# Results of the first five pairs of experts: to DRAM by slot and fetched by token, in place of products with the table of places

## The chip, the cores and the metric

The kernel runs on one core of one Trainium2 chip. The metric is the device time of one execution in microseconds (us), the median of several runs; lower is better. On the core, TensorE (PE in the profile) multiplies matrices, VectorE (DVE), ScalarE (ACT) and GpSimd (POOL) work element by element, and SyncE (SP) issues most transfers. Transfers run on 16 DMA engines. Those that SP issues are queue q1 in the profile, those that POOL issues are q0.

## The reference

The model has two layers. Each has a mixer (attention and gated linear attention), which the change does not touch, and a mixture of experts over 512 tokens of 1024 numbers. For each token a router chooses one of 4 groups and in it 2 of 8 experts, with a weight for each. What matters here is the sum over the experts:

```python
comb = (jax.nn.one_hot(grp_idx[:, 0], N_GROUPS, dtype=f32)[:, :, None]
        * exp_w[:, None, :]).astype(h.dtype)
y = jnp.zeros_like(hf)
for g in range(N_GROUPS):
    a = jnp.einsum('nd,edf->nef', hf, w_gate[g])
    u = jnp.einsum('nd,edf->nef', hf, w_up[g])
    y = y + jnp.einsum('nef,efd->nd', jax.nn.silu(a) * u * comb[:, g, :, None], w_down[g])
```

Afterwards x + gate_f * y is the input of the next layer or the output. All is float32. Each of the 32 experts of a layer has 3 MiB of weights (gate, up and down), 96 MiB in a layer. 512 tokens make 1024 choices of an expert.

## The kernel before

The mixture is `moe`. Each expert has 64 places (slots) for tokens; expert e's place s is slot 64e + s. The experts go in 16 pairs, 128 slots each, and pair i holds slots 128i to 128i + 127. The stage has these steps for pair i; the names in brackets are the tiles under which the profile lists them.

- `fetch` (L977, tile `rows`): POOL issues an indirect transfer of the normed token rows of the pair from DRAM, by a list of tokens for each slot. Empty slots have an index that is out of bounds and are left out.
- `gather` (L997, tile `g`): PE transposes the rows, and ACT and DVE scale them into `gT`.
- `hidden` (tiles `gu`, `hs`): 16 products of 64 columns against 512, for both experts of the pair, then silu and a product. Written below as gu(i).
- `turn` (L1032, tile `hsT`): PE transposes `hs`, ACT copies it to `hT`.
- `down` (tile `d`): 8 products with the down weights, d(i). DVE multiplies by the weight of the slot and by gate_f (L1057, tile `o`); ACT rounds this to a high part (L1062, `ohi`), and POOL makes the rest (L1063, `olo`).
- `places` (L1080, L1082): DVE makes the table `oT`, which has a one where a token holds a slot of the pair.
- `combine`: for each of 8 units (4 blocks of 128 tokens by 2 halves of 512 columns) PE multiplies the table with `ohi` and `olo` (tile `y`, L78), and DVE adds the result to x (L1070). So a pair has 16 products `y` and 8 additions, whatever number of tokens it holds.

The loop over i issues, for each pair, d(i-1), then gu(i), then the 8 units of pair i-1, between which lie the transposes of a later gather and the `turn` of pair i. The last two pairs are combined together in `combine_last`. PE's order around this is the program's (`pm` and `keep_in_program_order`); on DVE, ACT and POOL a scheduler may move instructions.

Weights come through two sets of buffers: 5 of 2 MiB (gate and up of one expert, tile `wgu`, L884) and 4 of 1 MiB (down, tile `wd`, L880). SP issues the loads in one fixed order, and a load waits at the head of SP's queue until the products that read its buffer are done. Nine loads are issued before the stage begins. After gu(0) come gate and up of experts 5 and 6, whose buffers gu(0) gives back, then down of experts 4 and 5, whose buffers d(0) gives back, and so on in the same manner. The last three are gate and up of expert 31, and down of experts 30 and 31.

`overflow_lists` (L1147 to L1176) prepares lists for experts with more than 64 tokens; it is issued after gu(1). In this data no expert has more, and the loop that would serve them runs no time.

Of the kernel before, what the change touches and what calls it, by code (L numbers as in the profile page):

```python
# [9 lines left out]
F = mybir.dt.float32  # L10
R = mybir.dt.float32r
BF = mybir.dt.bfloat16
I32 = mybir.dt.int32
# [7 lines left out]
P = 128  # L21
# [2 lines left out]
SBW, GKW, GVW, RANK, NIN = 512, 256, 512, 16, 3088  # L24
NE, FE, CAP = 32, 256, 64
NX = 16


@with_exitstack
def hybrid_decoder_kernel(ctx, tc, x, c, w_ada, b_ada, norm_mix, norm_ffn, w_in, w_gk2, b_gk, q_gain,  # L30
# [180 lines left out]

    xs = dram.tile([S, D], F, name="xs")
    xg = dram.tile([S, D], F, name="xg")

    mod = [const.tile([P, 6, KT], F, name=f"mod{l}") for l in range(L)]
    gates, gms, rowt = {}, {}, {}
# [643 lines left out]
    def moe(l, xt, ss, pool):  # L860
# [176 lines left out]
        def down(hT, ws, i=None):  # L1037

            n = len(ws)
            r = slice(0, 64 * n)  # L1040
            parts, last = [], None
            if i == NE // 2 - 1:

                last = wgu([P, 2, 2, 512], R, name="last")
            for q in range(2):
                pd = bank("d", "dy", 4)
                for j in range(2):
                    for e in range(n):
                        pm(pd[64 * e:64 * e + 64], hT[:, j, 64 * e:64 * e + 64],
                           ws[e][:, D * j + 512 * q:D * j + 512 * q + 512], j == 0, j == 1)  # L1050
                o = ot([P, 512], name="o")
                gate = gates[l, 5][r, 512 * q:512 * q + 512]
                if i is None:
                    V.tensor_tensor(o[r], pd[r], gate, op=OP.mult)
                    parts.append(o)
                else:
                    V.scalar_tensor_tensor(o, pd, cws[:, i:i + 1], gate, op0=OP.mult, op1=OP.mult)  # L1057
                    if last is not None:
                        hi, lo = last[:, q, 0], last[:, q, 1]
                    else:  # L1060
                        hi, lo = ohl([P, 512], R, name="ohi"), ohl([P, 512], R, name="olo")
                    A.activation(hi, o, AF.Copy)  # L1062
                    (G if last is None else V).tensor_tensor(lo, o, hi.bitcast(F), op=OP.subtract)  # L1063
                    parts.append((hi, lo))
            return parts
# [29 lines left out]
        def combine_last(pairs):  # L1095

            order = [units[u] for u in (0, 2, 4, 6, 1, 3, 5, 7)]
            tags = [("dy", 4), ("dy", 4), ("g", 2), ("g", 2), ("gu", 1), ("misc", 1), ("dy", 4), ("dy", 4)]
            ps = {}

            def unit(n, u):
                tt, q = order[u]
                if n == 0:
                    ps[u] = bank("y", *tags[u])
                oT, parts = pairs[n]
                for j in range(2):
                    pm(ps[u], oT[:, P * tt:P * tt + P], parts[q][j], n == 0 and j == 0, n == 1 and j == 1)
                if n:
                    add(tt, q, ps[u], True)

            for u in range(5):
                unit(0, u)
            yield
            for n, u in ((0, 5), (0, 6), (1, 0), (1, 1), (0, 7), (1, 2), (1, 3), (1, 4), (1, 5), (1, 6), (1, 7)):
                unit(n, u)

        def spread(slot, slot0):

# [80 lines left out]
        with tc.issue_after(listed.ins), tc.issue_after(normed.ins):  # L1199
# [14 lines left out]
            V.tensor_tensor(e2, e2, den, op=OP.mult)  # L1214
            V.tensor_tensor(cw[:, :, 1:2], e2, gw, op=OP.mult)
            dump(f"cw{l}", cw)
            exw = tmp.rearrange("p t k e -> p (t k) e")
            V.tensor_tensor(exw, ex.rearrange("p t k e -> p (t k) e"), cw.rearrange("p t k -> p (t k)")[:, :, None].to_broadcast([P, NT * 2, NE]), op=OP.mult)
        cws = pool.tile([P, NE // 2], F, name="cws")
# [17 lines left out]
        for _ in rest:  # L1237
            pass
        gT1, second = gather(fetched[1:2])
        hs = None  # L1240
        for i in range(NE // 2):
            while not {(0, 2 * i), (0, 2 * i + 1)} <= set(loaded):
                load_weights(1)
            if i % 2 == 0:
                now = gT
                if i < NE // 2 - 2:
                    gT, rest = gather(fetched[i + 2:i + 4])
                    fetched += [fetch(idx[:, j:j + 1]) for j in range(i + 4, min(i + 6, NE // 2))]

            if i:  # L1250
                part = places(i - 1), down(hT, [loaded.pop((1, e)) for e in (2 * i - 2, 2 * i - 1)], i - 1)
            *_, hs = hidden(gT1 if i == 1 else now, 0 if i < 2 else P * (i % 2), [loaded.pop((0, e)) for e in (2 * i, 2 * i + 1)])
            load_weights(4)
            if i == 1:
                overflow_lists()
            if i == NE // 2 - 1:
                break

            if i == 0:
                for _ in second:  # L1260
                    pass
                weights_by_slot()
            for u in range(4):
                for v in range(2):
                    if i:
                        combine(2 * u + v, *part)
                next(rest, None)
                if u == 2:
                    hT = turn(hs)
        last = []  # L1270
        end = combine_last([part, last])
        next(end)
# [93 lines left out]
```

## Time and profile before

| what | value |
|---|---|
| median of 3 runs | 1231.82 us (1229.91 to 1234.94) |
| the profiled execution | 1231.71 us, its span 1229.6 us |
| PE, DVE, ACT, POOL busy | 1176.4, 687.8, 472.6, 188.2 us |
| moved by DMA | 312.27 MB, mean 254 GB/s over the span |
| the expert stage, layer 0 | first gu at 375.15 us, last at 606.74 us |
| the expert stage, layer 1 | first gu at 969.53 us, last at 1201.12 us |

The page's second part cuts the span in 40 slices of 30.7 us. A busy PE says only that matmuls were under way; whether PE or the transfers set the pace is read from who waits for whom, and from the share of the 16 DMA engines in the same stretch. The GB/s of a slice counts all that moved.

### The profile page before, as it was taken

To read this page: it belongs to the slowest core of one execution; us is meant where nothing else is said; L and a number is where in the kernel's file an instruction comes from. 1 tells how busy PE (TensorE), PEld (TensorE's weight loads), DVE (VectorE), ACT (ScalarE), POOL (GpSimd) and SP (SyncE) were. 2 spreads that over 40 slices of the span, in tenths; PEclk is the share of its full clock that TensorE was granted. 3 is DMA by queue.
4 is the path that set the end of the run, shared out by engine and by line. 5 is a ranking of instruction groups with operands and counts; after the bars stand their busy time and mean duration, and the time that the engine had idled before them with its cause. 6 is when DMAs were issued, how large, how long until landed. Compare 5 with 4: busy or idle time off the path is not lost. (4 is left out here: it accounts for less than half of the span.)

```text
span 1229.6 us, 17212 instructions
## 1 busy us (share of the span) xinstructions
PE 1176.4 (96%) x6441; PEld 743.4 (60%) x6441; DVE 687.8 (56%) x1343; ACT 472.6 (38%) x940; POOL 188.2 (15%) x222
## 2 busy tenths in 40 slices
PE   4999999999989999999999997999999999999996
PEld 2687766666765444444478785666776744444443
DVE  4475545465864555555566563445846565555553
ACT  4376646453242111111155764454624411111111
POOL 1000010011302222221110001001310222222110
PEclk8999999999999999999999999999999999999999
DMA  9653665643687999999445354564129599999981
GB/s 299 211 181 110 202 166 155 198 152 96 258 353 265 410 411 420 420 419 418 178 168 167 96 172 108 171 179 127 56 103 383 212 397 420 420 418 420 420 328 69
DMA packets 105902, 312.27 MB, mean 254 GB/s; under 512 B 12852, under 2 KB 49912, under 8 KB 81240
## 3 DMA queue, kind: packets, MB, share of 16 engines
q1 hardware_dynamic: 96920, 289.62, 63.3%
q0 software_dynamic: 8896, 21.52, 5.2%
q8 instruction: 52, 0.85, 0.3%
q14 instruction: 34, 0.28, 0.1%
HBM read 311.08 MB, written 8.40 MB: 260 GB/s over the span
## 5 line engine op out<-in xcount | busy, mean ns | idle before, releaser
L78 PE MATMUL gu<-wgu,gT 128*64 128x512 f32 x1024 | 225.4, 592 | 0.1
L74 PE MATMUL proj<-whl,hh 128*128 128x512 f32 (+2 forms) x768 | 220.6, 370 | 0.1
L78 PEld LDWEIGHTS gu<-wgu,gT 128*64 128x64 f32 x1024 | 75.4, 137 | 143.7 <-issue 142.2
L74 PEld LDWEIGHTS proj<-whl,hh 128*128 128x128 f32 x768 | 133.9, 190 | 35.0 <-issue 13.3
L1070 DVE TENSOR_TENSOR x<-y,x 128x512 f32<-128x512 f32 x240 | 148.2, 679 | 0.9 <-PE y L78 0.9
L74 PE MATMUL proj<-whl,hl 128*128 128x512 f32 (+2 forms) x384 | 138.6, 362 | 0.0
L1025 DVE TENSOR_TENSOR hs<-hs,gu 128x256 f32<-128x256 f32 x32 | 13.5, 421 | 201.2 <-ACT hs L1024 201.2
L78 PE MATMUL d<-wd,hT 128*64 128x512 f32 x512 | 116.9, 598 | 1.4 <-ACT hT L1034 1.4
L1063 POOL TENSOR_TENSOR olo<-o,ohi 128x512 fp32r<-128x512 f32 x60 | 77.0, 1285 | 263.4 <-ACT ohi L1062 263.4
L96 DVE TENSOR_TENSOR whl<-raw,whl 128x512 fp32r<-128x512 f32 (+2 forms) x128 | 73.2, 574 | 78.0 <-ACT whl L95 67.6
L78 PE MATMUL y<-ohi,oT 128*128 128x512 f32 x240 | 104.5, 436 | 0.0
L95 ACT ACTIVATE whl<-raw 128x512 fp32r<-128x512 f32 (+2 forms) x128 | 66.4, 524 | 76.6 <-PE proj L74 64.7
L78 PE MATMUL y<-olo,oT 128*128 128x512 f32 x240 | 94.2, 393 | 0.0
L74 PEld LDWEIGHTS proj<-whl,hl 128*128 128x128 f32 x384 | 72.4, 189 | 14.2 <-issue 4.3
L1024 ACT ACTIVATE hs<-gu 128x256 f32<-128x256 f32 x32 | 12.3, 385 | 168.4 <-PE gu L78 168.4
L78 PEld LDWEIGHTS d<-wd,hT 128*64 128x64 f32 x512 | 33.9, 136 | 62.2 <-issue 48.1
L78 PEld LDWEIGHTS y<-ohi,oT 128*128 128x128 f32 x240 | 45.4, 189 | 31.7 <-issue 26.0
L1003 ACT ACTIVATE gT<-g,mod 128x256 f32<-128x256 f32 (+1 forms) x72 | 39.0, 544 | 62.6 <-DVE gT L1005 62.3
L1062 ACT ACTIVATE ohi<-o 128x512 fp32r<-128x512 f32 x60 | 37.8, 630 | 61.7 <-DVE o L1057 61.7
L1057 DVE SCALAR_TENSOR_TENSOR o<-d,cws,gate_f 128x512 f32<-128x512 f32 x64 | 47.6, 746 | 21.4 <-PE d L78 21.4
L733 POOL TENSOR_TENSOR raw<-raw,gate_m 128x1024 f32<-128x1024 f32 x16 | 40.4, 2533 | 122.9 <-DMA raw<-in_w_out_dram 63.1
L78 PE MATMUL ada<-wada,ct 128*32 128x512 f32 x320 | 50.2, 600 | 5.3 <-DMA wada<-in_w_ada_dram 3.8
(332 smaller groups left out, 1935.0 us busy)
## 6 DMA issues: line engine op xcount, KB each, us to landing
wgu<-in_w_gate_dram SPq DMA_DIRECT2D x64, 1024.0 KB, 9.6
wgu<-in_w_up_dram SPq DMA_DIRECT2D x64, 1024.0 KB, 11.8
wd<-in_w_down_dram SPq DMA_DIRECT2D x64, 1024.0 KB, 11.0
wada<-in_w_ada_dram SPq DMA_DIRECT2D x96, 512.0 KB, 5.1
raw<-in_w_in_dram SPq DMA_DIRECT2D x80, 256.0 KB, 4.5
raw<-in_w_out_dram SPq DMA_DIRECT2D x16, 512.0 KB, 5.0
raw<-in_w_in_dram SPq DMA_DIRECT2D x32, 128.0 KB, 4.0
xg<-xn POOLq DMA_DIRECT2D x8, 512.0 KB, 5.9
```

The source lines that it names most:

```text
L74: T.matmul(o, a, b, start=start, stop=stop, skip_group_check=True)
L78: tc.keep_in_program_order(T.matmul(o, a, b, start=start, stop=stop, skip_group_check=True))
L95: A.activation(hi, src, AF.Copy)
L96: eng.tensor_tensor(lo, src, hi.bitcast(F), op=OP.subtract)
L733: G.tensor_tensor(t, t, gates[l, 2][:, None, cols].to_broadcast([P, 2, 512]), op=OP.mult)
L1003: A.activation(o, src, AF.Identity, scale=m, bias=b)
L1024: A.activation(hs[r], gu[r, 0:256], AF.Silu)
L1025: V.tensor_tensor(hs[r], hs[r], gu[r, 256:512], op=OP.mult)
L1057: V.scalar_tensor_tensor(o, pd, cws[:, i:i + 1], gate, op0=OP.mult, op1=OP.mult)
L1062: A.activation(hi, o, AF.Copy)
L1063: (G if last is None else V).tensor_tensor(lo, o, hi.bitcast(F), op=OP.subtract)
L1070: V.tensor_tensor(xc, ps, xc, op=OP.add)
```

## The change

The outputs `o` of pairs 0 to 4 (NY = 5) are no longer split into two parts and multiplied with the table of places. POOL writes them to a DRAM tensor `ys` of 640 rows, row = slot, in two transfers of 128 rows of 2 KB for each pair. Near the end of the stage (from pair 12 on) POOL fetches rows of `ys` by token: for each block of 128 tokens and each of the 2 choices one indirect transfer into `back`, 8 in a layer. A choice whose slot is 640 or more is out of bounds and is left out. DVE then adds `back` times a mask (`ysm`, 1 or 0) to x, 128x1024 at a time.

The order of the first pairs changes with it: gu(i) comes first, then `turn` of pair i-1, 8 transposes, then d(i-1).

```diff
+NY = 5
...
+    ys = dram.tile([NY * P, D], F, name="ys")
...
-                o = ot([P, 512], name="o")
+                o = (ohl if i is not None and i < NY else ot)([P, 512], name="o")
...
                     V.scalar_tensor_tensor(o, pd, cws[:, i:i + 1], gate, op0=OP.mult, op1=OP.mult)
+                    if i < NY:
+                        kept_dma(G, ys[P * i:P * i + P, 512 * q:512 * q + 512], o)
+                        continue
...
+        ysi, ysm = pool.tile([P, NT, 2], I32, name="ysi"), t3(2, "ysm")
+
+        def take_back(tt, k):
+
+            r = rows_([P, D], name="back")
+            G.indirect_dma_start(r, None, ys[:, :], bass.IndirectOffsetOnAxis(ap=ysi[:, tt, k:k + 1], axis=0),
+                                 bounds_check=NY * P - 1, oob_is_err=False)
+            xc = xt[tt // 2][:, tt % 2]
+            return lambda: V.scalar_tensor_tensor(xc, r, ysm[:, tt, k:k + 1], xc, op0=OP.mult, op1=OP.add)
...
+            V.tensor_scalar(ysi, slot, 65535.0, None, op0=OP.min)
+            V.tensor_scalar(ysm, slot, float(NY * P), None, op0=OP.is_lt)
...
-            if i:
+            if i > NY:
                 part = places(i - 1), down(hT, [loaded.pop((1, e)) for e in (2 * i - 2, 2 * i - 1)], i - 1)
-            *_, hs = hidden(gT1 if i == 1 else now, 0 if i < 2 else P * (i % 2), [loaded.pop((0, e)) for e in (2 * i, 2 * i + 1)])
+            *_, new = hidden(gT1 if i == 1 else now, 0 if i < 2 else P * (i % 2), [loaded.pop((0, e)) for e in (2 * i, 2 * i + 1)])
             load_weights(4)
...
+            if i <= NY:
+                if i:
+                    hT = turn(hs)
+                for _ in range(4):
+                    next(rest, None)
+                if i:
+                    down(hT, [loaded.pop((1, e)) for e in (2 * i - 2, 2 * i - 1)], i - 1)
+                hs = new
+                if i == NY:
+                    hT = turn(hs)
+                continue
+            hs = new
             for u in range(4):
                 for v in range(2):
-                    if i:
-                        combine(2 * u + v, *part)
+                    combine(2 * u + v, *part)
+                if i >= NE // 2 - 4 and u % 2 == 0:
+                    taken.append(take_back(*back.pop(0)))
+                    if len(taken) > 1:
+                        taken.pop(0)()
                 next(rest, None)
                 if u == 2:
                     hT = turn(hs)
+        for (tt, k) in back:
+            taken.append(take_back(tt, k))
+        for add_back in taken:
+            add_back()
```

The order of SP's instructions is the same in both kernels, and outside the expert stages no engine's order changes. Three places matter below. The first is PE at the start of the stage, from gu(0) on. Before:

```order
L78 MATMUL gu<-wgu,gT 64x512 x16
L997 MATMUL g<-ident,rows 128x128 x8
L78 MATMUL lst<-tmp,ohp 64x16 x16
L78 MATMUL slots<-dg,n_72 128x128 x8
L997 MATMUL g<-ident,rows 128x128 x6
L1032 MATMUL hsT<-ident,hs 128x128 x2
L997 MATMUL g<-ident,rows 128x128 x2
L78 MATMUL d<-wd,hT 64x512 x8
L78 MATMUL gu<-wgu,gT 64x512 x16
```

In the changed kernel the same stretch, up to gu(2):

```order
L80 MATMUL gu<-wgu,gT 64x512 x16
L1000 MATMUL g<-ident,rows 128x128 x8
L80 MATMUL lst<-tmp,ohp 64x16 x16
L80 MATMUL slots<-dg,n_72 128x128 x8
L1000 MATMUL g<-ident,rows 128x128 x8
L80 MATMUL gu<-wgu,gT 64x512 x16
L1035 MATMUL hsT<-ident,hs 128x128 x2
L1000 MATMUL g<-ident,rows 128x128 x8
L80 MATMUL d<-wd,hT 64x512 x8
L80 MATMUL gu<-wgu,gT 64x512 x16
```

The first `d`, which gives back two `wd` buffers, now stands behind gu(1) instead of ahead of it.

The second place is POOL near the end of the stage of layer 0, from the third of the new fetches on; a number behind a name tells instances apart. olo_4932 and olo_4943 belong to pair 12, olo_5047 and olo_5058 to pair 13, the last two to pair 14. Before, this stretch held the six `olo` alone.

```order
L1128 DMA back_4981<-ys_125,ysi_3539 128x1024
L1069 TENSOR_TENSOR olo_4932<-o_4929,ohi_4931 128x512
L1069 TENSOR_TENSOR olo_4943<-o_4940,ohi_4942 128x512
L1128 DMA back_5010<-ys_125,ysi_3539 128x1024
L1128 DMA back_5089<-ys_125,ysi_3539 128x1024
L1128 DMA back_5110<-ys_125,ysi_3539 128x1024
L1128 DMA back_5174<-ys_125,ysi_3539 128x1024
L1069 TENSOR_TENSOR olo_5047<-o_5044,ohi_5046 128x512
L1069 TENSOR_TENSOR olo_5058<-o_5055,ohi_5057 128x512
L1128 DMA back_5178<-ys_125,ysi_3539 128x1024
L1069 TENSOR_TENSOR olo_5140<-o_5137,ohi_5139 128x512
```

Six of the eight fetches stand among the `olo` of the last pairs. The third, fourth, seventh and eighth (back_4981, back_5010, back_5174, back_5178) wait for a buffer that DVE gives back when it has added the first, second, third and fourth.

The third place is DVE from the places of the tokens (`pos`) to the list of tokens (`idx`), on which the first fetch depends. Before:

```order
L960 TENSOR_REDUCE pos<-tmp 128x8
L963 SCALAR_TENSOR_TENSOR slot<-eid,pos 128x8
L964 TENSOR_SCALAR far<-pos 128x8
L1181 TENSOR_TENSOR ohp<-iota,pos 128x512
L965 SCALAR_TENSOR_TENSOR slot<-far,slot 128x8
L1155 TENSOR_TENSOR cq<-pos,thr 128x56
L1229 TENSOR_TENSOR dg<-ident,slot 128x512
L972 TENSOR_SCALAR idx<-nv 128x16
```

In the changed kernel:

```order
L963 TENSOR_REDUCE pos<-tmp 128x8
L1163 TENSOR_TENSOR cmp<-n_e,thr 128x224
L966 SCALAR_TENSOR_TENSOR slot<-eid,pos 128x8
L967 TENSOR_SCALAR far<-pos 128x8
L1197 TENSOR_TENSOR ohp<-iota,pos 128x512
L968 SCALAR_TENSOR_TENSOR slot<-far,slot 128x8
L1165 TENSOR_REDUCE extra<-cmp 128x32
L1247 TENSOR_TENSOR dg<-ident,slot 128x512
L975 TENSOR_SCALAR idx<-nv 128x16
```

`cmp` now stands ahead of `ohp`, and the rest of `overflow_lists` with the two new instructions (`ysi`, `ysm`) follows between `idx` and the first `gT`; before, `overflow_lists` lay behind gu(0).

## Rows read from the trace of the kernel before

**Rows 1.** The page's second part: the span in 40 slices, busy tenths of PE and of the DMA engines, and GB/s.

```profile
PE   4999999999989999999999997999999999999996
DMA  9653665643687999999445354564129599999981
GB/s 299 211 181 110 202 166 155 198 152 96 258 353 265 410 411 420 420 419 418 178 168 167 96 172 108 171 179 127 56 103 383 212 397 420 420 418 420 420 328 69
```

**Rows 2.** Busy time by stretch: start and end, length, then PE, PEld, DVE, ACT and POOL busy (x instructions), granted PE clock, share of the DMA engines, GB/s.

```profile
400.00:450.00 50.00, 50.00 (x243) 24.60 (x243) 29.68 (x52) 9.99 (x20) 11.69 (x10) 1.00 1.00 411
450.00:500.00 50.00, 50.00 (x242) 23.27 (x240) 28.92 (x52) 10.35 (x20) 12.03 (x11) 1.00 1.01 419
500.00:550.00 50.00, 50.00 (x241) 23.12 (x238) 26.20 (x46) 9.79 (x19) 11.87 (x10) 1.00 1.01 419
540.00:580.00 40.00, 40.00 (x194) 18.75 (x194) 23.58 (x42) 8.77 (x17) 7.66 (x6) 1.00 1.01 420
340.00:345.00 5.00, 5.00 (x25) 4.14 (x24) 2.72 (x5) 2.83 (x8) 0.00 (x0) 1.00 1.04 434
1220.00:1224.00 4.00, 0.31 (x2) 0.00 (x0) 2.12 (x4) 0.00 (x0) 0.00 (x0) 1.00 1.03 377
```

**Rows 3.** Waits, 370 to 610 us: all of PE's, then the two longest of SP's queue (300 to 600 us): who, for whom, us in total, times, longest.

```profile
PE g L997 <- DMA rows<-xg,idx: 0.8, 1, 0.8
PE d L78 <- ACT hT L1034: 0.2, 1, 0.2
...
SPq L884 <- PE gu L78: 109.9, 14, 33.7
SPq L880 <- PE d L78: 93.0, 14, 7.8
```

**Rows 4.** PE in order of time (start, length, instructions, count): the start of the stage, then pair 3 up to gu(4), and the last gu.

```profile
382.23 1.09 PE L997 MATMUL g<-ident,rows 128*128 128x128 f32 x8
386.84 0.40 PE L1032 MATMUL hsT<-ident,hs 128*128 128x128 f32 x2
387.70 3.65 PE L78 MATMUL d<-wd,hT 128*64 128x512 f32 x16 [0.24 <-ACT hT L1034]
391.19 7.04 PE L78 MATMUL gu<-wgu,gT 128*64 128x512 f32 x32
...
422.11 7.04 PE L78 MATMUL gu<-wgu,gT 128*64 128x512 f32 x32
429.07 0.50 PE L78 MATMUL y<-ohi,oT 128*128 128x512 f32 x1
434.08 3.65 PE L78 MATMUL d<-wd,hT 128*64 128x512 f32 x16
437.57 7.04 PE L78 MATMUL gu<-wgu,gT 128*64 128x512 f32 x32
...
606.74 7.04 PE L78 MATMUL gu<-wgu,gT 128*64 128x512 f32 x32
```

**Rows 5.** SP's issues in order of time: the first loads that wait for a buffer, and the last gate and up.

```profile
382.26 0.33 SPq L884 DMA_DIRECT2D wgu<-in_w_gate_dram  x1
391.38 0.80 SPq L880 DMA_DIRECT2D wd<-in_w_down_dram  x2
...
584.15 0.42 SPq L884 DMA_DIRECT2D wgu<-in_w_up_dram  x1
```

**Rows 6.** Transfers by issue: how many, KB each, median us from issue to landing. First those issued from 382 to 390 us, then from 391 to 398, from 530 to 537, and from 583 to 586.

```profile
wgu<-in_w_up_dram SPq DMA_DIRECT2D x2, 1024.0 KB, 9.6
...
wd<-in_w_down_dram SPq DMA_DIRECT2D x2, 1024.0 KB, 6.4
...
wd<-in_w_down_dram SPq DMA_DIRECT2D x2, 1024.0 KB, 12.5
...
wgu<-in_w_up_dram SPq DMA_DIRECT2D x1, 1024.0 KB, 10.0
```

**Rows 7.** DMA queues from 400 to 580 us: packets, MB, share of 16 engines; and the fetches issued there.

```profile
q1 hardware_dynamic: 9945, 72.48, 97.2%
q0 software_dynamic: 1440, 2.41, 3.6%
...
rows<-xg,idx POOLq DMA_INDIRECT x10, 9.5
```

**Rows 8.** DVE in order of time at the start of the stage (start, length, what, idle before and until what).

```profile
365.55 0.42 DVE L960 TENSOR_REDUCE pos<-tmp 128x8 f32<-128x256 f32 x1
366.16 0.69 DVE L1181 TENSOR_TENSOR ohp<-iota,pos 128x512 f32<-128x512 f32 x1
369.92 0.43 DVE L1218 TENSOR_TENSOR tmp<-ex,cw 128x256 f32<-128x256 f32 x1
374.68 1.78 DVE L1005 TENSOR_SCALAR gT<-g,mod 128x128 f32<-128x128 f32 x4 [4.33 <-PE g L997]
386.52 0.38 DVE L1147 TENSOR_TENSOR cmp<-n_e,thr 128x224 f32<-128x224 f32 x1
392.38 0.17 DVE L1167 TENSOR_SCALAR over<-over 128x8 f32<-128x8 f32 x1
```

**Rows 9.** The page's fifth part: one line's additions to x.

```profile
L1070 DVE TENSOR_TENSOR x<-y,x 128x512 f32<-128x512 f32 x240 | 148.2, 679 | 0.9 <-PE y L78 0.9
```

**Rows 10.** Stretches around a lull of PE ahead of the stage, columns as in Rows 2.

```profile
355.00:360.00 5.00, 2.60 (x13) 1.48 (x13) 2.41 (x9) 2.95 (x2) 0.50 (x1) 1.00 1.01 393
360.00:365.00 5.00, 4.52 (x35) 4.25 (x34) 4.30 (x21) 3.40 (x3) 1.09 (x3) 0.66 0.90 366
365.00:370.00 5.00, 4.63 (x63) 4.42 (x61) 4.31 (x22) 1.49 (x2) 0.42 (x1) 1.00 0.26 106
```

More of the change, by code (lines that the diff above doesn't have):

```diff
@@ L1239, in moe @@
         gT1, second = gather(fetched[1:2])
-        hs = None
+        hs, back, taken = None, [(tt, k) for tt in range(NT) for k in range(2)], []
         for i in range(NE // 2):
@@ L1262, in moe @@
                 weights_by_slot()
+            if i <= NY:
[9 more added lines that the diff above has]
+                continue
+            hs = new
             for u in range(4):
                 for v in range(2):
-                    if i:
-                        combine(2 * u + v, *part)
+                    combine(2 * u + v, *part)
[3 more added lines that the diff above has]
+                        taken.pop(0)()
                 next(rest, None)
```

## The prediction

> **What bounds the kernel now.** I read the page's second part first. In slices 13 to 19 and again in slices 33 to 38 (a slice is 30.7 us) PE is at 9 and the DMA engines are at 9 as well, with 410 to 420 GB/s [rows 1]. These are the two expert stages, and the change touches nothing else. The table of stretches says the same more sharply: from 400 to 550 us PE is busy 50.00 of 50 us and the share of the 16 DMA engines is 1.00 to 1.01 [rows 2]. So two resources are full at once, and the question is which has room. The list of waits answers for PE: from 370 to 610 us it waited 1.0 us in all, while SP's loads waited 203 us for PE's products to give buffers back [rows 3]. PE leads, and the weights follow. PE's rows give the pace: pair 3 from gu to gu takes 437.57 - 422.11 = 15.46 us [rows 4].
>
> But the weights follow closely. A pair needs 6 MiB, 6.29 MB; at the 420 GB/s of 540 to 580 us, which holds hardly anything but weights [rows 2], that is 15.0 us, and a fetch of rows costs more on top. The two loads of down weights issued at 391 us landed after 6.4 us, those issued at 530 us after 12.5 us [rows 6]: a backlog of some 6 us grew over the stage. The room that is left shows at the end: the up weights of expert 31 were issued at 584.15 us and took 10.0 us [rows 5, 6], so they were there at 594.2, and gu(15) read them from 606.74 [rows 4]. That is a slack of 12.6 us per layer, and it is all that PE can win before the weights are late.
>
> **The change part by part**, for layer 0; layer 1 repeats it.
>
> PE. A pair without products y saves this: from the end of gu(3) to d(3) it is 434.08 - 429.07 = 5.01 us [rows 4], and without the 16 y there remain 8 transposes (1.1 us for 8 by the row at 382.23) and a turn, 1.3 us together. That saves 3.7 us a pair, 18.5 us for five. If PE alone set the time, two layers would give 37 us.
>
> The weights at the start. PE's order shows d(0) moved behind gu(1). Before, d(0) ended at 391.2 and SP issued down of experts 4 and 5 at 391.38 [rows 4, 5]. Now gu(1) begins at 386.84 + 0.4 = 387.2 (where hsT stood, with two transposes left), takes 6.96 (422.11 to 429.07), then turn and transposes 1.3, d(0) 3.49 (387.70 to 391.19): it ends at 398.9 and the load is issued at 399.1. All later loads stand behind it in SP's order, so the freed gate and up buffers don't help. What is in flight meanwhile is gate and up of experts 5 and 6, issued from 382.26: the median landing of 9.6 us [rows 6] puts their end at about 393 to 394. Two down loads, 2.10 MB or 5.0 us at 420 GB/s, landed 6.4 us after issue, so bytes begin 1.4 us after the issue, now at 400.5. The engines, which before had no gap here, stand idle from 394 to 400.5, less 0.7 for a fetch that falls in it: 5.8 us. Bounds: 4 (another fetch and the first writes fill part) and 7.8 (the whole delay of the issue).
>
> The writes. Five pairs write 5 x 128 x 1024 x 4 bytes = 2.62 MB. The nearest row is the writing of the output, also rows of 2 KB from SBUF to DRAM: 377 GB/s at a share of 1.03 [rows 2]. That is 7.0 us; bounds 6.2 (at 420) and 8.0 (at 326, next paragraph).
>
> The fetches by token. From 400 to 580 us q0 moved 2.41 MB in a share of 3.6% of 180 us, 6.5 us; or, by what the weights leave (72.48 MB at 420 GB/s are 172.6 us), in 7.4 us [rows 7]. So 371 or 326 GB/s, 0.65 to 0.74 us for each of the 10 fetches. The new ones bring back the choices that fall on 10 of 32 experts, some 320 of 1024, if the experts share evenly: 1.31 MB, an estimate, 4.0 us at 326. Bounds: 3.1 (at 420) and 5.9 (8 times 0.74).
>
> These transfers are issued by another engine than the weights. In the row of queues the shares of q1 and q0 add up to 100.8% [rows 7], so I count their time in full. The Trainium skill ("DMA: Bandwidth & Descriptors", section on issuing engines not being separate queues) says that transfers started by scalar, sync or gpsimd run on the same 16 engines and interleave; the trace agrees, and by this rule the change adds to the resource that is full.
>
> DVE, ACT, POOL. 40 additions of 679 ns [rows 9] go, 27 us, and 8 additions of twice the width come, about 1.4 us each by that row, 11 us. All engines but PE have room (DVE 29.68 of 50 us [rows 2]), so this is worth nothing. At the front `cmp`, 0.38 us [rows 8], now stands between pos and ohp: +0.3 us. The rest of overflow_lists, some 3.5 us net of what lay between 386.52 and 392.55, moves into DVE's idle time of 4.33 us ahead of the first gT [rows 8]: nothing.
>
> The sum. The weights of expert 31 come later by 5.8 + 7.0 + 4.0 = 16.8 us, of which 12.6 are slack: gu(15) starts 4.2 us later, with the front 4.5 us. PE, 18.5 us ahead of its old time by itself, is held by weights, first at gu(3) or gu(4). Behind gu(15) the order is the old one; d(15)'s weights come one load pair (5 us) after gu(15)'s and are read 9 to 10 us after it starts. Two layers: +9 us. The profiled execution took 1231.71 us, the median of the runs is 1231.82, so the two can be read as one: 1231.7 + 9 = 1241 us. With all lower bounds (13.3 - 12.6 + 0.3 = 1.0 a layer) 1234; with all upper ones (21.7 - 12.6 + 0.3 = 9.4) 1250. Waits of PE may also lower its clock: after 355 to 360 us, with PE busy 2.60 of 5, the granted clock of the next 5 us was 0.66, and then 1.00 again [rows 10]. The waits I expect, of 3 to 7 us, lie in pairs 3 to 6, where PE waits for weights anyway; so I count nothing.
>
> **The rivals.**
> - The engines carry more when more is queued. For it: 434 GB/s in one stretch of 5 us [rows 2]. Against: three stretches of 50 us at full share held 411 to 419 with 6 to 12 us of loads queued. The bytes from down of expert 4 to up of expert 31 are 79.7 MB; at 434 they take 6.1 us less than at 420, so a layer changes by 4.5 - 6.1 = -1.6 us: 1228. The Trainium skill ("DMA: Bandwidth & Descriptors", Specifications) puts the fabric's ceiling at 435 GB/s; no long stretch of this trace reaches it, and by that figure the rival would come out about here.
> - Writes and fetches fit beside the weights and cost them nothing, since another queue carries them. Then only the gap counts, 5.8 - 12.6 + 0.3 = -6.5 a layer: 1219; at the far end, with the weights never late, 1195. Against it stands the share of 1.00 to 1.01, for it nothing but the mean under 1.00 at the ends of the stage.
> - The fetches by token hold POOL. The third waits for DVE's addition of the first, the seventh for that of the third, and behind the seventh stand the olo of pair 13, for which PE waits. Fetches land in 9.5 us now [rows 7], and by the pace of 15.46 us a pair this chain is done with some 10 us to spare; it decides once a landing takes about 20 us. At 25 us each layer loses 5 us for the chain more: 1251.
>
> **How the numbers follow.** The weights bind and the new bytes exceed the slack: 0.55, own range 1234 to 1250; 0.46 of it slower, 0.09 inside 0.5%. More bytes a second: 0.20, of which 0.16 unchanged, 0.04 faster. New transfers for nothing: 0.13, 0.10 faster and 0.03 unchanged. POOL held: 0.12, slower. What a measurement of this kernel can tell from no change is about 0.5%, 6 us. So faster 0.14, same 0.28, slower 0.58. The range 1227 to 1250 leaves out the far end of the second rival and the worst of the third.
>
> **What would show it.** Right: PE's waits name the transfers of wgu, first about gu(3), 15 to 20 us of them in a layer in the cheap pairs; a dip of the DMA share between 394 and 400 us, and then a share of 1.00 to the end of the stage; landings of weights at 20 us or more; gu(15) near 611 us. Wrong: gu(15) ahead of 603, GB/s well over 420 with PE not waiting, or waits of PE that name POOL's olo at pairs 12 to 14.

## The result, and the profile after

The changed kernel takes 1239.94 us (median of 5 runs, 1238.09 to 1245.04); the kernel before, timed beside it, takes 1232.63 us. The ratio is 1.0076, with a 95% interval from 1.0055 to 1.0097. The profiled execution of the changed kernel took 1238.09 us, its span is 1236.3 us.

First the busy tenths in 40 slices and GB/s of the page; a slice is 30.9 us, and slices are counted from 0. They answer to [rows 1].

```profile
PE   4999999999999889999999997999999997999996
PEclk9999999999989989999999998999999998999998
DMA  9653665553676999999755354563239589999992
GB/s 302 220 165 129 183 175 171 169 179 115 271 303 225 411 421 421 419 419 419 307 185 158 87 198 81 171 187 120 69 129 401 200 342 420 421 420 419 419 415 96
```

The transfers are as full as before in slices 13 to 18 and 33 to 38, and no fuller: 411 to 421 GB/s. New is PE, at 8 in slices 13 and 14 and at 7 in slice 33, with a granted clock of 8 tenths in slices 14 and 33. PE now waits at the start of the stage. For what, the table of waits says (us in total, times, longest), first 370 to 625 us and then, after the line of dots, 960 to 1225 us. It answers to [rows 3], where PE waited 1.0 us:

```profile
PE gu L80 <- DMA wgu<-in_w_up_dram: 10.3, 3, 4.8
PE y L80 <- POOL olo L1069: 2.0, 1, 2.0
PE d L80 <- ACT hT L1037: 1.0, 2, 0.5
PE gu L80 <- DVE gT L1008: 0.7, 1, 0.7
...
PE gu L80 <- DMA wgu<-in_w_up_dram: 11.0, 3, 6.7
PE y L80 <- POOL olo L1069: 2.1, 1, 2.1
PE gu L80 <- DVE gT L1008: 1.2, 1, 1.2
```

PE in order of time shows where (compare [rows 4]; the bracket is the wait before a row and what ended it):

```profile
373.13 7.16 PE L80 MATMUL gu<-wgu,gT 128*64 128x512 f32 x32 [0.66 <-DVE gT L1008]
...
393.81 3.65 PE L80 MATMUL d<-wd,hT 128*64 128x512 f32 x16
...
413.69 8.75 PE L80 MATMUL gu<-wgu,gT 128*64 128x512 f32 x30 [3.62 <-DMA wgu<-in_w_up_dram]
...
430.04 7.05 PE L80 MATMUL gu<-wgu,gT 128*64 128x512 f32 x30 [1.85 <-DMA wgu<-in_w_up_dram]
...
447.65 9.06 PE L80 MATMUL gu<-wgu,gT 128*64 128x512 f32 x30 [4.83 <-DMA wgu<-in_w_up_dram]
...
475.97 0.50 PE L80 MATMUL y<-olo,oT 128*128 128x512 f32 x1 [1.98 <-POOL olo L1069]
483.78 7.04 PE L80 MATMUL gu<-wgu,gT 128*64 128x512 f32 x32
...
607.43 7.92 PE L80 MATMUL gu<-wgu,gT 128*64 128x512 f32 x32
```

The waits are at gu(3), gu(4) and gu(5), each behind the first two products. After the two longer waits the rest of gu takes 8.75 and 9.06 us, after the shortest 7.05. From gu(7) at 483.78 PE runs at 15.48 us a pair, up to gu(13). The last gu takes 7.92 us instead of 7.04, and the profile names no wait in it; experiments 1, 2 and 7 point to the last up weights, which land at about that moment. By stretch (columns as in [rows 2]) the cause of the early waits is ahead of them:

```profile
390.00:395.00 5.00, 5.00 (x28) 2.20 (x26) 1.42 (x3) 1.64 (x4) 0.95 (x1) 1.00 0.51 215
395.00:400.00 5.00, 5.00 (x26) 1.71 (x24) 1.50 (x2) 0.14 (x1) 2.21 (x4) 1.00 0.64 170
400.00:405.00 5.00, 5.00 (x28) 1.90 (x25) 0.20 (x1) 0.58 (x2) 0.00 (x0) 1.00 0.94 303
405.00:410.00 5.00, 5.00 (x24) 1.74 (x22) 2.66 (x5) 1.20 (x3) 0.54 (x1) 1.00 1.00 423
...
440.00:450.00 10.00, 5.17 (x18) 1.57 (x16) 1.50 (x2) 0.00 (x0) 1.08 (x2) 0.74 1.02 425
...
500.00:550.00 50.00, 50.00 (x242) 23.19 (x240) 26.05 (x46) 9.77 (x19) 11.68 (x10) 1.00 1.02 419
...
605.00:610.00 5.00, 5.00 (x24) 1.60 (x21) 5.00 (x7) 0.70 (x2) 1.21 (x1) 1.00 0.90 370
```

The DMA engines are half idle from 390 to 400 us: SP issued a load at 381.57 us and the next, for the buffers that d(0) gives back, at 397.49. From 405 us on they are full to the end of the stage. From 440 to 450 us, around the longest wait, the granted clock of PE was 0.74.

Where the time went, from rows of PE and of the last addition, in us, before and after:

| stretch | layer 0 | layer 1 |
|---|---|---|
| lists of tokens (tile `nv`) to gu(0) | 8.16, 8.53 | 7.85, 8.30 |
| gu(0) to gu(15) | 231.59, 234.30 | 231.59, 234.54 |
| gu(15) to the next layer, or to the end | 19.03, 19.92 | 28.48, 30.73 |

These add up to 9.6 us. Of the 0.89 us behind the start of gu(15) in layer 0, 0.88 are gu(15) itself (7.92 against 7.04); the 2.25 us of layer 1 lie behind the last addition (9.73 against 7.48 us to the end of the span). The profiled executions differ by 6.4 us only, since what lies outside the two stages came out 3.2 us shorter in this one execution.

### The profile page after: what moved, and what is told of

Read it like the earlier page. It is cut to its first block, busy times and chain, and to the rows that moved or that the text cites. A ratio compares the mean times of both kernels' runs of the same rounds, so it can differ in the third digit from the quotient of the medians.

```text
span 1236.3 us, 16854 instructions
## 1 busy us (share of the span) xinstructions
PE 1156.6 (94%) x6281; PEld 722.6 (58%) x6281; DVE 656.5 (53%) x1263; ACT 458.9 (37%) x920; POOL 193.4 (16%) x238
## 5 line engine op out<-in xcount | busy, mean ns | idle before, releaser
L80 PE MATMUL gu<-wgu,gT 128*64 128x512 f32 x1024 | 239.4, 607 | 23.2 <-DMA wgu<-in_w_up_dram 21.3
L76 PE MATMUL proj<-whl,hh 128*128 128x512 f32 (+2 forms) x768 | 220.2, 370 | 0.1
L80 PEld LDWEIGHTS gu<-wgu,gT 128*64 128x64 f32 x1024 | 81.3, 140 | 173.8 <-issue 161.0
L1076 DVE TENSOR_TENSOR x<-y,x 128x512 f32<-128x512 f32 x160 | 99.8, 680 | 4.7 <-PE y L80 4.7
L1069 POOL TENSOR_TENSOR olo<-o,ohi 128x512 fp32r<-128x512 f32 x40 | 53.9, 1350 | 124.6 <-ACT ohi L1068 109.8
L80 PE MATMUL y<-ohi,oT 128*128 128x512 f32 x160 | 70.0, 437 | 0.4 <-DVE x L1076 0.4
L80 PE MATMUL y<-olo,oT 128*128 128x512 f32 x160 | 63.2, 395 | 4.1 <-POOL olo L1069 4.1
L980 POOL DMA_INDIRECT rows<-xg,idx x32 | 32.7, 1022 | 147.9 <-PE g L1000 131.8
L527 DVE SCALAR_TENSOR_TENSOR t<-z,t 128x384 f32<-128x384 f32 (+1 forms) x48 | 28.6, 600 | 39.5 <-ACT t L526 37.7
```

The source lines that it names most:

```text
L76: T.matmul(o, a, b, start=start, stop=stop, skip_group_check=True)
L80: tc.keep_in_program_order(T.matmul(o, a, b, start=start, stop=stop, skip_group_check=True))
L527: V.scalar_tensor_tensor(t[:, w], z[:, w], 0.0, t[:, w], op0=OP.max, op1=OP.add)
L980: G.indirect_dma_start(r, None, xg[:, :], bass.IndirectOffsetOnAxis(ap=idx, axis=0), bounds_check=S - 1, oob_is_err=False)
L1076: V.tensor_tensor(xc, ps, xc, op=OP.add)
```

## The experiments

Theory A is the prediction's: the weights bind, they come later by the gap at the start and by the new transfers, less a slack of 12.6 us a layer. Its check is one quantity, how long after gu(0) the up weights of expert 31 have landed, beside the start of gu(15), which reads them. The other theories (A1, B, R2, R3) are explained in the expectation in which they first stand. Every ratio below is against the kernel before, timed beside it.

**1. The gap.** `e1_first_down_early` puts d(0) back ahead of gu(1).

```diff
+            if i == 1:
+                down(hT, [loaded.pop((1, e)) for e in (0, 1)], 0)
             if i > NY:
...
-                if i:
+                if i > 1:
                     hT = turn(hs)
                 for _ in range(4):
                     next(rest, None)
-                if i:
+                if i == 0:
+                    hT = turn(new)
+                if i > 1:
```

> The changed kernel, with d(0) put back ahead of gu(1) (turn of pair 0 follows the 8 transposes behind gu(0)); all else, the bytes too, is that of the changed kernel. Theory A (the weights bind, and the gap of the transfers at the start of the stage is part of the loss): the DMA share no longer falls between 390 and 400 us, the weights of all later experts come 5.8 us earlier, PE waits about 4 to 6 us less for wgu in a layer, and the time falls by 2 x 5.8 = 11.6 us from 1239.9 to about 1228, under the kernel before (1232.6). Theory A1 (the gap is taken up later by PE's own losses, so part of it only returns): 1231 to 1236. Rival B (the gap costs nothing; the loss is in the new transfers and the engines at the end of the stage): 1239 to 1241.

Measured: 0.9996 (0.9976 to 1.0016), against 1.0076; so some 10 us less. By stretch:

```profile
385.00:390.00 5.00, 4.54 (x23) 1.57 (x24) 3.15 (x6) 1.29 (x3) 0.61 (x1) 1.00 1.03 429
390.00:395.00 5.00, 5.00 (x26) 1.64 (x24) 0.05 (x1) 0.00 (x0) 0.56 (x1) 1.00 1.00 381
395.00:400.00 5.00, 5.00 (x28) 2.54 (x26) 1.33 (x3) 1.40 (x3) 2.08 (x2) 1.00 1.01 425
```

The gap is closed, and PE's waits for wgu are 4.7 and 6.0 us (10.3 and 11.0 before). gu(15) starts 5.0 and 5.6 us earlier after gu(0), so 10.6 of A's 11.6 us came back. The profiled executions differ by 12.8 us; most of the rest lies ahead of gu(0), 0.8 and 1.15 us, where PE no longer waits for gT. `overflow_lists` (its last row is tile `xei`) ends ahead of the first gT in both kernels; what differs is that DVE makes its first four gT two and two in the changed kernel and in a row here. DVE in the changed kernel, then here:

```profile
370.70 0.18 DVE L1192 CAST xei<-xe 128x17 int32<-128x17 f32 x1
372.67 0.73 DVE L1008 TENSOR_SCALAR gT<-g,mod 128x128 f32<-128x128 f32 x2 [1.79 <-PE g L1000]
...
372.33 1.78 DVE L1008 TENSOR_SCALAR gT<-g,mod 128x128 f32<-128x128 f32 x4 [1.06 <-PE g L1000]
```

Rival B falls. The time alone, some 10 us less, does not part A from A1. SP's issue of the last up weights, their landing (median us), and gu(15):

```profile
579.51 0.33 SPq L887 DMA_DIRECT2D wgu<-in_w_up_dram  x1
...
wgu<-in_w_up_dram SPq DMA_DIRECT2D x1, 1024.0 KB, 22.7
...
602.07 7.30 PE L80 MATMUL gu<-wgu,gT 128*64 128x512 f32 x32
```

They land at 602.2 us, just after gu(15) began, and gu(15) takes 0.26 us more than its 7.04.

**2. The transfers taken out.** `e2_no_fetch` leaves out the fetches and their additions; `e3_no_write_no_fetch` the writes too.

```diff
-        hs, back, taken = None, [(tt, k) for tt in range(NT) for k in range(2)], []
+        hs, back, taken = None, [], []
...
                     if i < NY:
-                        kept_dma(G, ys[P * i:P * i + P, 512 * q:512 * q + 512], o)
                         continue
```

(The first edit alone is the kernel without fetches.)

> The changed kernel without the 8 fetches by token and without the 8 additions of what they bring: the outputs of the first five pairs are written to ys and are missing from the result (and the tokens of layer 1 fall on its experts a little differently). Theory A as on record (the fetches' bytes count in full, 4.0 us a layer): 1239.9 - 8 = 1232. Theory A1 (weights bind only up to gu(5), and the PE losses behind it leave a slack in which the fetches run): 0 to 2 us a layer, 1236 to 1240. Rival R3 (the fetches hold POOL and DVE at the end of the stage): a layer gains the wait of the last pairs and a shorter tail, 2 us or more, 1234 to 1236, with PE waits for olo gone and the tail from gu(15) to the end about 1 us shorter, while the weights land as before.

> As the kernel without the fetches, and the 10 writes to ys in a layer are left out too: the outputs of the first five pairs are computed and dropped. What it differs by from the kernel without fetches is the price of the writes. Theory A and A1 (writes run in the pairs where PE waits for weights and count in full, 7.0 us a layer; five writes of the last pair's buffers also hold ohi, 2.0 us of PE in a layer, which lies beside the weights): 10 to 14 us less than the kernel without the fetches, about 1222 to 1226. Rival R2 (another queue carries them for nothing): no more than 2 us less.

Measured: 1.0032 (1.0013 to 1.0052) without fetches, 0.9895 (0.9864 to 0.9925) without both. From gu(0) to gu(15) the kernel without fetches is 2.2 and 1.6 us a layer shorter than the changed kernel, and in layer 0 gu(15) itself takes 7.04 us instead of 7.92; the end of the program is 0.8 us shorter. A1's range fits this, A's 4.0 a layer does not. But it is not the price of the fetches. The last up weights of this kernel in layer 0:

```profile
585.62 0.33 SPq L887 DMA_DIRECT2D wgu<-in_w_up_dram  x1
...
wgu<-in_w_up_dram SPq DMA_DIRECT2D x1, 1024.0 KB, 19.9
```

They are there 585.62 + 19.9 - 374.90 = 230.6 us after gu(0), and gu(15) starts at 232.1; in layer 1 it is 231.3 and 232.9. So without the fetches gu(15) is no longer held by them, and PE's own losses early in the stage set its time. Leaving out the writes gives another 17 us (14.2 by the profiled executions), where A had 10 to 14: 5.4 and 7.1 us from gu(0) to gu(15), where A has 7.0, and 1.5 us once at the program's end, which no theory had. R2 falls: the writes are paid.

**3. The transfers added to the kernel before.** In `e4_products_and_bytes` products and order are those of the kernel before, and the writes, fetches and additions (masked to zero) come on top. `e6_products_and_double_writes` writes each output twice.

```diff
                     V.scalar_tensor_tensor(o, pd, cws[:, i:i + 1], gate, op0=OP.mult, op1=OP.mult)
+                    if i < NY:
+                        kept_dma(G, ys[P * i:P * i + P, 512 * q:512 * q + 512], o)
+                        kept_dma(G, ys2[P * i:P * i + P, 512 * q:512 * q + 512], o)
...
+            V.tensor_scalar(ysm, slot, -1.0, None, op0=OP.is_lt)
```

(The line with ys2 is in the second kernel alone; `take_back` is that of the change.)

> The kernel before, products y and order untouched, with the new transfers on top: o of pairs 0 to 4 is also written to ys, and fetched by token from pair 12 on; the fetched rows are added with a mask of zeros. Theory A (the transfers' 11 us a layer are weights that come later, and PE has 12.6 us of slack where it is not made faster): PE still does not wait for wgu, or under 1 us; 1233 to 1236 with the additions and a longer tail. Rival R3 (the fetches and additions at the end of the stage hold POOL, DVE and PE whatever the weights do): 1238 or more. Rival R2 (transfers for nothing): 1232 to 1234, and gu(15)'s up weights land as early as before.

> The kernel before with the new transfers on top, as in the kernel with products and bytes (1.0043 of the kernel before), but each output of pairs 0 to 4 is written twice, to two tensors. Theory A with the prices on record: 14 + 4 = 18 us of transfers a layer against a slack of 12.6, so PE waits 5.4 us a layer for wgu in the late pairs; with the price as the kernel with products and bytes has it (9.3 us where 11.0 were counted) 15.2, and 2.6 us a layer. Against the kernel before: +5 us as there, +5 to +11 for the waits, +1.5 for 20 more transfers at the program's end: 1.009 to 1.014. Rival R2 (transfers beside the weights for nothing): no wait for wgu, 1.004 to 1.006.

Measured: 1.0043 (1.0025 to 1.0062) and 1.0107 (1.0089 to 1.0125). With one write PE does not wait for wgu; with two it waits, at gu(15). SP's issue of the last up weights and their landing (median us), first with one write, then PE with two:

```profile
579.72 0.42 SPq L886 DMA_DIRECT2D wgu<-in_w_up_dram  x1
...
wgu<-in_w_up_dram SPq DMA_DIRECT2D x1, 1024.0 KB, 18.9
```

```profile
586.26 0.33 SPq L887 DMA_DIRECT2D wgu<-in_w_up_dram  x1
...
wgu<-in_w_up_dram SPq DMA_DIRECT2D x1, 1024.0 KB, 22.9
...
609.32 7.05 PE L79 MATMUL gu<-wgu,gT 128*64 128x512 f32 x30 [1.59 <-DMA wgu<-in_w_up_dram]
```

So the weights of expert 31 are there 579.72 + 18.9 - 370.32 = 228.3 us after gu(0) with one write, 586.26 + 22.9 - 373.43 = 235.7 with two, and 584.15 + 10.0 - 375.15 = 219.0 before [rows 4 to 6]. Writes and fetches together cost 9.3 us, the second set of writes 7.4, and 9.2 us in layer 1 for the first two. That would leave 1.9 for the fetches if both sets of writes cost the same. They need not: the first set found transfers that were not quite full. From 400 to 450 us they moved 411 GB/s before [rows 2]; in the same stretch after gu(0), here 395 to 445 us, they now moved 421:

```profile
395.00:445.00 50.00, 50.00 (x243) 24.68 (x244) 29.89 (x52) 10.00 (x20) 15.24 (x16) 1.00 1.02 421
```

That is room for 1.2 us of the new transfers. The slack swallows 9.3 and not 16.7; PE's waits of 1.6 and 1.2 us with two writes are below the 2.6 and 5.4 on record. A's forecast for the kernel with one write (1233 to 1236 beside 1232.6, 1.000 to 1.003) was too low all the same: a pair takes 16.14 us instead of 15.46 from gu(13) to gu(14), where the fetched rows are added, and the end of the program is 2.4 us longer. This much of R3 is true, and R3's time (1238 or more, a ratio of 1.0044) fits as well; that PE does not wait for wgu, and that SP's last loads land 9.3 us later all the same, speaks for A.

**4. Neither gap nor transfers.** `e5_no_gap_no_bytes` joins the edits of 1 and 2.

> The changed kernel with d(0) put back ahead of gu(1), and without the writes and the fetches: the outputs of the first five pairs are computed and dropped. Only the cheaper pairs are left of the change. Theory A: PE can win no more than the slack of the weights, 12.6 us a layer, though it saves 18.5; it still waits for wgu, some 4 to 6 us a layer, and the time is 2 x 12.6 = 25 us under the kernel before (1230.6 on the last chip): about 1205, and about 12 us under the kernel with the gap and without the transfers (1217). Rival (PE alone sets the time once nothing is added to the transfers): 37 us under the kernel before, about 1194, and no waits for wgu.

Measured: 0.9866 (0.9845 to 0.9887), 16.5 us under the kernel before. The rival, 37 us, falls, but A's 25 us is missed too. From gu(0) to gu(15) the gain is 8.8 and 6.7 us a layer. In layer 0 the up weights of expert 31, issued at 576.88 us with a landing of 19.9, are there 220.2 us after gu(0) at 376.62, and gu(15) starts at 222.8, so 2.6 us of the slack are not used. PE still waits 4.2 and 5.0 us for wgu, early in the stage; after the longest wait a gu takes 10.02 us instead of 7.04:

```profile
428.99 8.75 PE L80 MATMUL gu<-wgu,gT 128*64 128x512 f32 x30 [3.07 <-DMA wgu<-in_w_up_dram]
444.61 7.05 PE L80 MATMUL gu<-wgu,gT 128*64 128x512 f32 x30 [1.12 <-DMA wgu<-in_w_up_dram]
...
1028.46 10.02 PE L80 MATMUL gu<-wgu,gT 128*64 128x512 f32 x30 [4.70 <-DMA wgu<-in_w_up_dram]
...
1030.00:1035.00 5.00, 5.00 (x16) 1.42 (x14) 0.00 (x0) 0.00 (x0) 0.00 (x0) 0.56 1.01 423
```

The last row is a stretch with columns as in [rows 2]: behind the longest wait the granted clock was 0.56.

The slack at the end of the stage is an upper bound: PE spends its gain early, is held there, and what it loses then by waits and clock is not won back.

**5. Fewer pairs.** `e7_two_pairs` and `e8_three_pairs` are the kernel of experiment 1 with another constant.

```diff
-NY = 5
+NY = 2
```

> The changed kernel with d(0) put back ahead of gu(1), and only two pairs (NY = 2) go by slot and token. Theory A: transfers of 2/5 x 11.0 = 4.4 us leave 8.2 us of the slack, more than the 7.4 us that PE saves, so PE is not held by the weights and keeps its gain, less 0.7 at gu(13), 0.9 behind gu(15), 2.0 for ohi behind the writes, and 1.5 once at the program's end: 2 x 3.8 - 1.5 = 6 us under the kernel before, 0.995 of it (0.990 to 0.997), faster than the kernel with five pairs and the same order (0.9996). Rival (the gain goes with the number of pairs: fewer pairs, less gain): 0.9998 or slower.

> As the kernel with two pairs, with NY = 3. Theory A: PE saves 11.1 us a layer, transfers of 6.6 us leave 6.0 of the slack, so the weights hold PE for some us in a layer again; 2 x (6.0 - 1.6) - 1.6 = 7 us under the kernel before, 0.994 (0.988 to 0.997), within 2 us of the kernel with two pairs. Rival (PE alone sets the time): 2 x (11.1 - 3.6) - 1.6 = 13 us under, 0.989, and no waits for wgu.

Measured: 0.9933 (0.9915 to 0.9952) with two pairs and 0.9945 (0.9927 to 0.9964) with three, both faster than the kernel before and than five pairs in the same order (0.9996). With two pairs PE does not wait for wgu at all; with three 0.2 us, though some gu are a few tenths longer. Both rivals fall. For three pairs A's time came out, but its reason only in small part: PE gained 6.3 and 4.1 us from gu(0) to gu(15) (4.9 and 4.9 with two pairs). What can be the weights is about 1 us in layer 0, the 0.2 and two pairs that are 0.4 longer, and nothing in layer 1. PE also waited 1.2 and 2.4 us for olo at the first pair with products, and behind the longer of these waits the granted clock was 0.72 from 1030 to 1035 us.

**6. The overflow lists.** In `f3_lists_late` they are held behind gu(0)'s hs in the changed kernel; `f1_two_pairs_lists_late` and `f2_three_pairs_lists_late` do so with two and three pairs.

```diff
-                overflow_lists()
+                with tc.issue_after(made[0].ins):
+                    overflow_lists()
```

(`made` holds the product that makes hs.)

> The changed kernel (1.0076 of the kernel before) with this one edit: the overflow lists held behind gu(0)'s hs. PE's wait for gT at gu(0) (0.7 and 1.2 us) goes, and so the first loads that gu(0) and d(0) free are issued as much earlier. Theory A (the weights bind from d(0)'s loads to the end of the stage): 1 to 1.5 us less a layer, 2 to 3 us in all, 1.005 to 1.006. Rival (the cheap pairs have PE waiting anyway, so the front costs nothing): 1.0076, and the waits for wgu longer by what gu(0) comes earlier.

> The kernel with two pairs and d(0) ahead of gu(1) (0.9933), with the overflow lists held behind gu(0)'s hs, as they stood in the kernel before. There PE waited 0.6 and 1.3 us for gT ahead of gu(0), and cmp stood ahead of ohp. If those waits are part of the path: 1 us less in layer 0 and 1.5 us in layer 1, 2 to 3 us in all, 0.991 of the kernel before, about 1220. Rival (the front is taken up later, as the weights catch up): no change against 0.9933.

> The kernel with three pairs and d(0) ahead of gu(1) (0.9945), with the overflow lists held behind gu(0)'s hs. Both theories as for two pairs: 2 to 3 us less (0.992), since an earlier gu(0) gives back its buffers earlier and so moves the weights too; or no change.

Measured: 1.0076 (1.0053 to 1.0100) with five pairs, so nothing, as its rival says, though the waits for wgu did not grow (8.0 and 8.7 us) and the lost time stands in longer pairs behind them. In layer 1 the last up weights land 1184.12 + 20.3 - 970.70 = 233.7 us after gu(0), and gu(15) starts at 236.8: there PE's early waits and its clock set the time, not these weights. Two pairs: 0.9925 (0.9903 to 0.9946), which cannot be told from 0.9933. Three pairs: 0.9914 (0.9897 to 0.9931) against 0.9945, whose intervals overlap. In all three PE's wait for gT is gone. That the lists cause it is not shown: in experiments 1, 2 and 7 they lie where they do in the changed kernel, and PE does not wait for gT either. That losing this wait is worth 2 to 3 us is likely with three pairs and not shown.

**7. The clock.** `g1_busy_while_waiting` keeps PE busy in the waits of the changed kernel.

```diff
+            if 3 <= i <= NY:
+                keep_warm(lo.rearrange("p t e -> p (t e)"), 10)
             *_, new = hidden(
```

> The changed kernel (1.0076 of the kernel before) with 10 idle products (tile warm, some 2.6 us) ahead of each of gu(3), gu(4) and gu(5), where PE waits 1.8 to 6.7 us for wgu; after the longer of these waits the granted clock fell and gu took 8.75 to 9.06 us instead of 7.04. The idle products lie in the waits, so PE's sequence is busy there. Theory A as on record (the weights bind to the end of the stage, so PE's clock in the cheap pairs costs nothing): the clock holds, gu keeps 7.04, PE waits for wgu less by about the idle products, and the time stays: 1.006 to 1.009. Rival (the slower clock is on the path): gu(0) to gu(7) is 3 to 5 us shorter in a layer and the time 6 to 10 us less, 1.000 to 1.003. If neither holds and the idle products delay the last loads' buffers: over 1.010.

Measured: 1.0073 (1.0050 to 1.0097). This run tells most. PE in order of time, and the last up weights:

```profile
413.90 7.05 PE L80 MATMUL gu<-wgu,gT 128*64 128x512 f32 x30 [0.82 <-DMA wgu<-in_w_up_dram]
...
430.87 7.05 PE L80 MATMUL gu<-wgu,gT 128*64 128x512 f32 x30 [1.38 <-DMA wgu<-in_w_up_dram]
...
448.15 7.05 PE L80 MATMUL gu<-wgu,gT 128*64 128x512 f32 x30 [1.69 <-DMA wgu<-in_w_up_dram]
...
513.81 7.05 PE L80 MATMUL gu<-wgu,gT 128*64 128x512 f32 x30 [0.71 <-DMA wgu<-in_w_up_dram]
...
608.70 7.05 PE L80 MATMUL gu<-wgu,gT 128*64 128x512 f32 x30 [0.94 <-DMA wgu<-in_w_up_dram]
...
585.75 0.33 SPq L887 DMA_DIRECT2D wgu<-in_w_up_dram  x1
...
wgu<-in_w_up_dram SPq DMA_DIRECT2D x1, 1024.0 KB, 22.8
```

The clock holds: gu takes 7.05 us behind each of these waits, and from gu(0) to gu(7) a layer is 3.2 us shorter than in the changed kernel. In layer 0 all of it is given back: PE waits for wgu again at gu(9) and at gu(15), and from gu(0) to the end of gu(15) it takes 242.1 us, against 242.2 in the changed kernel. The weights of expert 31 land 585.75 + 22.8 - 373.68 = 234.9 us after gu(0), 15.9 us later than before. In the changed kernel itself PE reached gu(15) after 234.3 us, at about that moment, and took 0.88 us too long for it, so there the waits and the slow clock early in the stage hid the same bound. In layer 1 the weights land 1180.27 + 21.5 - 968.40 = 233.4 us after gu(0), just after gu(15) began:

```profile
1201.10 7.84 PE L80 MATMUL gu<-wgu,gT 128*64 128x512 f32 x32
```

To the end of gu(15) layer 1 takes 240.5 us, against 241.6 in the changed kernel, so 1.0 of the 3.2 us is kept. The rival's 6 to 10 us fall; a gain of up to some 4 us could hide in the two intervals.

## Why the prediction was right

The time (1241 us forecast, 1239.94 measured) and the mechanism stand. That the two numbers lie so close is in part luck. Against the kernel before, 9 us were forecast and 7.3 measured; gu(15) starts less late than forecast, and 2.25 us lie at the program's end, where the forecast had nothing.

- **PE leads and the weights follow; 12.6 us of slack.** Right. Transfers of 9.3 us added to the kernel before make PE wait for nothing, 16.7 us do. That the slack "is all that PE can win" holds as a bound; 8.8 and 6.7 us of it could be won.
- **The gap at the start, 5.8 us.** Right: in layer 0 the last up weights land 234.9 us after gu(0) with the gap (experiment 7) and 579.51 + 22.7 - 372.80 = 229.4 without it (experiment 1), a difference of 5.5 us. In layer 1 it is 233.4 and 1171.39 + 21.3 - 963.57 = 229.1, so 4.3 us, near the lower bound. The dip lay at 390 to 405 us, where 394 to 400 was forecast.
- **The writes, 7.0 us.** Right: 7.4 us, by the kernel with double writes.
- **The fetches, 4.0 us.** Not refuted, and not settled. The subtraction in experiment 3 gives 1.9 us, on a condition that need not hold. Experiments 2 and 7, which differ in the idle products too, have the last up weights at 230.6 and 234.9 us, and at 231.3 and 233.4 in layer 1; by this the fetches cost 4.3 and 2.1 us. By the time of their packets they took 4.2 us: in experiment 7 the eight fetches moved 1.50 MB in 8.1% of the 51.6 us from 557 to 608.6, where the last up weights landed, and nothing of them was left for later. In layer 1 it was 1.33 MB in 3.8 us.

```profile
q0 software_dynamic: 1152, 1.50, 8.1%
```

- **The weights of expert 31 later by 16.8 us, gu(15) later by 4.2 us a layer.** 15.9 us in layer 0, and gu(15) starts 2.7 us later and ends 3.6 us later. In layer 1 the weights come 13.7 us later (233.4 in experiment 7 against 1178.53 + 10.7 - 969.53 = 219.7 before), the slack before was 11.9 us there, and gu(15) is 2.95 us later. The weights explain 1.8 of these; about 1.0 us is what PE's early waits and clock added, since experiment 7 has it back.
- **DVE, ACT and POOL worth nothing.** Wrong in small. The 8 additions make the pair from gu(13) 0.68 us longer (15.48 us without them, experiment 2). `cmp`, +0.3 in the sum, makes the way from pos to the lists of tokens 0.18 us longer (1.62 against 1.44 us). The rest of `overflow_lists` did fit into DVE's idle time, as forecast: 1.79 us of it are left. Not forecast are PE's waits of 0.7 and 1.2 us for gT; the way from the lists of tokens to gu(0) is 0.37 and 0.45 us longer.
- **Behind gu(15) the old order, so nothing.** Right up to the last addition: the 0.89 us of layer 0 lie in gu(15) itself, most likely a wait for its weights, since gu(15) takes 7.04 us where they land before it (experiment 2). Missed is the end of the program, 2.25 us more, a term that the forecast did not have.
- **PE's waits of 15 to 20 us in the cheap pairs.** 10.3 and 11.0 us. The rest went into slower products behind the waits and into 2.0 us for olo at pair 5, and experiment 7 shows that the clock and the waits lie beside the weights, but for 1.0 us in layer 1. That the clock may be counted at next to nothing was right for five pairs, and for the reason given. Where the last weights land well ahead of gu(15), as in experiments 4 and 6, it need not hold.
- **The rivals.** More bytes a second: no; no slice of some 31 us held over 424 GB/s in any run, with landings of up to 22.9 us. The Trainium skill ("DMA: Bandwidth & Descriptors", Specifications) has the fabric's ceiling at 435 GB/s; no such slice came to it. Transfers for nothing: no, by experiments 2 and 3. The Trainium skill ("DMA: Bandwidth & Descriptors", Issuing engines are not separate DMA queues) says that transfers of several issuers interleave on the same 16 engines; the second set of writes, issued by POOL, pushed SP's loads back by 7.4 us, so the trace agrees. POOL held: not by the named chain, whose landings were 8.9 us in the median; PE's waits for olo lie elsewhere, as follows.
- **A slip in reading.** The prediction has both resources full in slices 13 to 19 and 33 to 38; counted from 0, [rows 1] has them so in 13 to 18 and 33 to 37. Nothing rests on it.

PE's 2.0 us for olo are at the first pair with products, pair 5. ACT in order of time shows why:

```profile
465.34 0.63 ACT L1068 ACTIVATE ohi<-o 128x512 fp32r<-128x512 f32 x1 [2.82 <-DVE o L1060]
472.75 0.63 ACT L1068 ACTIVATE ohi<-o 128x512 fp32r<-128x512 f32 x1 [6.79 <-DMA ys<-o]
```

The outputs of the cheap pairs lie in the four buffers that ohi and olo use, and pair 4's hold theirs until its writes, 11.7 us long, have landed; d(4) and d(5) follow each other directly in the new order.

## What to carry to other kernels

Where two resources are nearly full, work out the slack of the one that follows, as the time from a landing to its use, and charge every new byte and every later buffer against it. A gain on the leading engine is worth no more than that slack less what the edit adds, so it pays to do the edit only as often as the slack allows: with the old order of the first down two or three pairs gave 0.991 to 0.995 of the kernel before and five gave 0.9996; the changed kernel, with the gap on top, has 1.0076. That an engine waits does not show that removing the wait helps: kept busy in its waits, PE finished its last gu at the same time in one layer and 1.0 us earlier in the other.

## What was not expected of the hardware

- The end of the program grows with the new transfers. From the end of the last addition to the end of the span it is 7.48 us in the kernel before, 7.43 without writes and fetches, 7.47 and 7.72 with two and three pairs, 8.94 with five pairs' writes alone, 9.73 in the changed kernel, and 11.36 with double writes. In the changed kernel the last of the output is moved until about 1228.5 us, at 373 GB/s; from 1230.5 to 1236.3 us PE, DVE, ACT and POOL are not busy, and the share of the transfers is 0.03 and then 0.00. What fills this time was not tried.
- SP's loads, which before waited for PE's products alone, wait in the changed kernel for other loads too, by the profile. Why was not tried. From 370 to 610 us the largest such group is

```profile
SPq L887 <- DMA wd<-in_w_down_dram: 31.1, 16, 3.2
```

- Landings of 22.8 us (experiment 7), where 10.0 were seen before, did not raise the bytes a second: from 500 to 550 us 419 GB/s were moved in the kernel before, in the changed kernel and in experiment 7.
